# Side steps at every second dense step in three stretches of a four-branch encoder layer

## The chip, the cores and the metric

One core of one Trainium2 chip runs the whole program. The time is in device microseconds (us) of one execution; the number given for a kernel is the median of three runs. PE is TensorE (matmuls, with PEld its weight loads), DVE is VectorE, ACT is ScalarE, POOL is GpSimd, SP is SyncE, which issues the DMAs here.

## The reference

Two groups of 512 tokens (`x_prompt`, `x_sample`) go through the same two layers. In fp32, with D = 1024:

```
h = rms_norm(x, g_mix);  z = h @ w_in          # one projection, split into 15 parts
A = retention(rq, rk, rv) * silu(rg)           # 4 heads, chunks of 128, both directions
B = neighbourhood_attention(nq, nk, nv) * silu(ng)   # 8 heads, 8x16 window, learned bias
C = rg_lru(conv(lx)) * silu(lg)                # both directions
D = hgrn2(hq, hff, hfb, hi) * silu(hg)         # 4 heads, both directions
x = x + (sum over j of sigmoid(h @ w_mg[j]) * (branch_j @ w_br[j])) @ w_o
x = x + sigmoid(rms_norm(x, g_ple) @ w_pg) * (p @ w_pp)
```

After the second layer a last RMSNorm gives the two outputs.

## The kernel before

The kernel makes four passes through `layer`: group 0 and group 1 through layer 0, then both through layer 1. Activations lie with their channels on the partitions, 128 by 512 a tile. Every fp32 operand of a large product is split into a high and a low part (`split`, L246: ACT writes `hi`, DVE writes `lo`), and a product is three matmuls (`mm3`, L275). Weights come as units of 128 by 1024 (512 KB): `weights` (L261) issues the DMA into `wr` (two buffers) and splits it into `wh` by ACT and `wl` by DVE (three buffers each). One unit feeds 24 matmuls of 512 columns; half of it, 12 matmuls, is a dense step.

The order of PE's instructions is the order in which the program issues them (`manual_schedule` for PE, L1239). The order on ACT, DVE, POOL and SP is set when the program is built, by a scheduler with its own estimate of times; each of these engines then works through its list in that order.

Branches are generators that yield after each step. `mix` (L1078) runs a dense generator, and after each of its steps gives every side generator a credit; a whole credit takes one side step. So `mix` writes PE's order. The parts that matter here, in one pass:

- `a_proj` (L611) is dense: `vproj` (eight steps, RV, its units two steps each) and four `ztile` units for q and k, 16 steps in all. Beside it runs `b_core` (L843), the core of branch B, at 1.15 steps to a dense step. One step of it has been taken before: the query tile of the first pair.
- `b_core` takes for each of four head pairs: the query tile and the key tile (`b_qk`, L749, 24 matmuls each, evicted from PSUM by ACT into the high part and by DVE into the low part of `nqk`), then the scores in two steps (`b_scores`, L773, 12 small matmuls each, which read both parts), and behind the second the softmax (`b_soft`, L793, on ACT and DVE). Transposes and value products of a pair (`b_pair`, L826) are taken between the steps of the next pair; for the first pair there is nothing between.
- `vproj` for HI and `c_proj` (L872) are dense, 16 steps; `b_core` goes on at 1.6.
- `merge` for branch B (L948, 24 dense steps) has `a_core` (L653) beside it at 1.0 and the first head of `d_core` (L509) at 0.35.

PSUM has four banks for dense tiles (`mm`) and four for side steps (`co`).

Of the kernel before, what the change touches and what calls it, by code (L numbers as in the profile page):

```python
# [91 lines left out]
class Trunk:  # L92
# [982 lines left out]
                    self.nc.sync.dma_start(out=self.dbg[name][n, i], in_=bo[n][:, i].bitcast(F32))  # L1075

    @staticmethod
    def mix(dense, *sides):  # L1078

        credit = [0.0] * len(sides)  # L1080
        for _ in dense:
            for i, (gen, rate) in enumerate(sides):
                credit[i] += rate
                while credit[i] >= 1.0:
                    credit[i] -= 1.0
                    next(gen, None)
# [7 lines left out]
    def layer(self, g, l, nxt, prev, start=None):  # L1094
        chain = itertools.chain
        sa, sb_, sc, sd = {}, {}, {}, {}
        a, b, c, d, dst = [], [], [], [], []
        self.mg, self.mhl = [None] * 8, [None] * 8

        if start is None:  # L1100
            self.mix(self.b_proj(l, sb_), (prev, 0.3))
        else:
            self.mix(self.b_proj(l, sb_, True), (start, 1.0))
            self.drain(start)
        bcore = self.b_core(l, sb_, b)
        next(bcore)
        self.mix(self.a_proj(l, sa), (bcore, 1.15), (prev, 0.7))
        self.mix(chain(self.vproj(l, C_HI, sd), self.c_proj(l, sc)), (bcore, 1.6), (prev, 0.7))
        self.drain(prev)
        self.drain(bcore)  # L1110
        self.show("B", b)
        acore = self.a_core(l, sa, a)
        self.mix(self.d_proj(l, 0, dst), (acore, 0.9))
        self.cops = {}
        self.c_fetch(l, 0, sc["X"])
        ccore = chain(*[self.c_tile(l, t, sc["X"], c) for t in range(4)])
        dcore = [self.d_core(l, n, dst, sd["V"], d) for n in range(4)]
        self.mix(self.merge(l, 1, b, True, False), (acore, 1.0), (dcore[0], 0.35))
        self.drain(acore)
        self.show("A", a)  # L1120
        self.mix(self.d_proj(l, 1, dst), (dcore[0], 1.0), (ccore, 0.62))
        self.mix(self.merge(l, 0, a, False, False), (chain(dcore[0], dcore[1]), 0.5), (ccore, 0.62))
        self.mix(self.d_proj(l, 2, dst), (chain(dcore[0], dcore[1]), 0.6), (ccore, 0.62))
        self.drain(dcore[0], ccore)
        self.show("C", c)
        self.mix(self.d_proj(l, 3, dst), (dcore[1], 0.6), (dcore[2], 0.4))
        self.mix(self.merge(l, 2, c, False, False), (chain(dcore[1], dcore[2]), 0.5), (dcore[3], 0.4))
        gt = []
        self.mix(self.gates(l, 3, gt), (chain(dcore[1], dcore[2], dcore[3]), 0.6))
        self.drain(*dcore)  # L1130
        self.show("D", d)
        self.mix(self.merge(l, 3, d, False, True, gt), (self.late, 1.0))
        self.drain(self.late)
        st = {}
        self.p_load(g, l, st)
        side = iter(()) if nxt is None else self.make_h(*nxt)
        self.mix(self.w_out(g, l, st), (side, 0.5))
        self.drain(side)
        self.drain(self.ple(g, l, st))
        return self.close(g, l, st)  # L1140
# [110 lines left out]
```

## Time and profile before

| | |
|---|---|
| median of three runs | 3078.2 us (3077.31 to 3078.43) |
| the profiled execution, its own time | 3077.61 us |
| its span, first to last instruction | 3075.8 us |
| mean granted TensorE clock | 0.996 |
| PE busy | 3038.0 us, 17940 matmuls |
| DVE, ACT, POOL busy | 1864.3, 1346.7, 635.5 us |

The profiled execution is one run with the profiler on. Its own time is 1.8 us above its span and 0.6 us under the median. A matmul of 512 columns is shown as 0.39 us long, while the next one starts 0.227 us later: their records overlap, so a busy share near 100% says only that PE is not idle. What a stretch takes is read from the start times. Four stretches of the trace repeat each other, one for each pass; they begin about 757 us apart.

### The profile page before, as it was taken

The page shows a single profiled execution, that of the slowest core. Times are in us where ns is not written, and L with a number is a line of the kernel's source. Part 1 is how long each engine was busy: PE and PEld are TensorE (multiplying, and loading weights), DVE is VectorE, ACT ScalarE, POOL GpSimd, SP SyncE. Part 2 cuts the span into 40 slices and gives each one's busy share as a digit, 9 for nine tenths or more (in the row PEclk, how much of TensorE's full clock was granted, in tenths as well). Part 3 has the DMA queues.
Part 4 walks back from the last instruction along what each step waited for, and adds up shares of the span by engine and source line. Part 5 has one row for each costly group of instructions (what it writes and reads, how often), then busy time and mean ns, then how long its engine had stood idle before and what let it go on. Part 6 is the DMA issues. An engine that isn't in the chain of part 4 may idle for free.

```text
span 3075.8 us, 44900 instructions
## 1 busy us (share of the span) xinstructions
PE 3038.0 (99%) x17940; PEld 2463.9 (80%) x17940; DVE 1864.3 (61%) x2864; ACT 1346.7 (44%) x2173; POOL 635.5 (21%) x486
## 2 busy tenths in 40 slices
PE   8999999999999999999999999999999999999997
PEld 6888877888888887788888887788887888778886
DVE  7556667457455665745646666574665666666446
ACT  4433464344343346433433335643453433564333
POOL 3102043232120113311112112231201211223120
PEclk9999999999999999999999999999999999999998
DMA  5423222244432222223443322222435332222232
GB/s 169 125 92 95 81 93 89 78 145 152 154 116 91 88 93 88 84 85 130 144 147 116 97 83 93 84 87 83 147 106 169 112 96 83 93 81 90 84 131 74
DMA packets 115105, 326.57 MB, mean 106 GB/s; under 512 B 20816, under 2 KB 25680, under 8 KB 114896
## 3 DMA queue, kind: packets, MB, share of 16 engines
q1 hardware_dynamic: 114896, 323.70, 32.4%
q8 instruction: 141, 2.31, 0.3%
q14 instruction: 68, 0.56, 0.1%
HBM read 298.48 MB, written 12.58 MB: 101 GB/s over the span
## 4 chain that ended last, share of the span: by engine, by line
PE 97%; DVE 1%; ACT 1%; DMA 1%; POOL 0%; issue 0%; SPq 0%; DVEq 0%; POOLq 0%; ACTq 0%
PE z L277 22%; PE z L278 22%; PE z L279 21%; PE bp L277 4%; PE bp L279 4%; PE bp L278 4%; PE v L277 3%; PE v L278 3%; PE v L279 3%; PE bo L821 1%; PE cg L912 1%; PE bs L785 1%; PE bt L809 1%; PE by L506 1%; PE ks L587 1%; PE ss L322 1%
## 5 line engine op out<-in xcount | busy, mean ns | idle before, releaser
L250 DVE TENSOR_TENSOR wl<-wr,wh 128x1024 fp32r<-128x1024 f32 x487 | 628.1, 1290 | 679.3 <-ACT wh L248 675.1
L248 ACT ACTIVATE wh<-wr 128x1024 fp32r<-128x1024 f32 x488 | 516.3, 1058 | 1090.2 <-PE z L278 773.1
L277 PE MATMUL z<-hh,wh 128*128 128x512 f32 x2432 | 967.7, 398 | 0.0
L278 PE MATMUL z<-hl,wh 128*128 128x512 f32 x2432 | 948.4, 390 | 2.4 <-DVE hl L250 2.4
L279 PE MATMUL z<-hh,wl 128*128 128x512 f32 x2432 | 948.8, 390 | 0.0
L277 PEld LDWEIGHTS z<-hh,wh 128*128 128x128 f32 x2432 | 457.0, 188 | 117.8 <-issue 22.2
L279 PEld LDWEIGHTS z<-hh,wl 128*128 128x128 f32 x2432 | 456.9, 188 | 96.9
L278 PEld LDWEIGHTS z<-hl,wh 128*128 128x128 f32 x2432 | 457.4, 188 | 92.1 <-DVE hl L250 2.8
L978 POOL TENSOR_TENSOR mg<-mg,mt 128x512 f32<-128x512 f32 x96 | 144.0, 1503 | 448.1 <-DVE mt L976 448.1
L544 POOL TENSOR_TENSOR K<-K,f 128x512 f32<-128x512 f32 x112 | 146.4, 1308 | 434.3 <-DVE f L548 314.6
L277 PE MATMUL v<-wh,hh 128*128 128x512 f32 x384 | 155.5, 405 | 8.2 <-ACT wh L248 8.2
L278 PE MATMUL v<-wl,hh 128*128 128x512 f32 x384 | 152.2, 396 | 0.5 <-DVE wl L250 0.5
L279 PE MATMUL v<-wh,hl 128*128 128x512 f32 x384 | 151.8, 395 | 0.0
L768 POOL TENSOR_TENSOR bm<-run,cmask 128x256 f32<-128x256 f32 x96 | 79.1, 858 | 318.8 <-DMA run<-rpb 203.0
L353 POOL TENSOR_TENSOR acc<-acc,sq 128x512 f32<-128x512 f32 x52 | 80.3, 1544 | 266.3 <-ACT sq L352 262.8
L545 DVE TENSOR_TENSOR Q<-Q,f 128x512 f32<-128x512 f32 x112 | 91.8, 819 | 67.9 <-PE by L506 20.9
L278 PE MATMUL z<-mhl,wh 128*128 128x512 f32 x256 | 100.0, 391 | 0.9 <-DVE mhl L252 0.9
L277 PE MATMUL z<-mhl,wh 128*128 128x512 f32 x256 | 100.0, 391 | 0.4
L277 PE MATMUL z<-h2h,wh 128*128 128x512 f32 x256 | 99.6, 389 | 0.0
L279 PE MATMUL z<-h2h,wl 128*128 128x512 f32 x256 | 99.6, 389 | 0.0
L279 PE MATMUL z<-mhl,wl 128*128 128x512 f32 x256 | 99.6, 389 | 0.0
L278 PE MATMUL z<-h2l,wh 128*128 128x512 f32 x256 | 99.6, 389 | 0.0
(254 smaller groups left out, 4628.5 us busy)
## 6 DMA issues: line engine op xcount, KB each, us to landing
wr<-wu SPq DMA_DIRECT2D x488, 512.0 KB
vb<-vs SPq DMA_DIRECT2D x32, 256.0 KB
run<-rpb SPq DMA_DIRECT2D x32, 244.5 KB
vs<-V SPq DMA_DIRECT2D x4, 1024.0 KB
sw<-raw SPq DMA_DIRECT2D x32, 128.0 KB
qq<-raw SPq DMA_DIRECT2D x32, 128.0 KB
xs<-X SPq DMA_DIRECT2D x32, 128.0 KB
xo<-xT SPq DMA_DIRECT2D x16, 256.0 KB
```

The costliest lines, as they stand in the source:

```text
L248: nc.scalar.activation(hi, src, AF.Copy, scale=scale)
L250: (eng or nc.vector).tensor_sub(lo, src, hi.bitcast(F32))
L277: t.matmul(out, lhsT=wh, rhs=xh, start=start, stop=False)
L278: t.matmul(out, lhsT=wh, rhs=xl, start=False, stop=False)
L279: t.matmul(out, lhsT=wl, rhs=xh, start=False, stop=stop)
L322: nc.tensor.matmul(c, lhsT=self.onesr, rhs=x, start=i == 0, stop=i == 1)
L353: (eng or nc.gpsimd).tensor_tensor(out=acc, in0=acc, in1=s, op=ALU.add)
L506: self.nc.tensor.matmul(bank[r0:r0 + 32, col + 32 * (b // 4):col + 32 * (b // 4) + 32], lhsT=kf(32 * b), rhs=qf(32 * b), start=True, stop= ...
L544: nc.gpsimd.tensor_tensor(out=kv, in0=kv, in1=tk, op=ALU.mult)
L545: nc.vector.tensor_tensor(out=qv, in0=qv, in1=tq, op=ALU.mult)
L768: nc.gpsimd.tensor_tensor(out=bm[:, ty].rearrange("p (r j) -> p r j", j=32), in0=self.view(run, 488 - off, [[-63, 8], [-1, 32]]), in1=self ...
L978: nc.gpsimd.tensor_add(self.mg[m], self.mg[m], dst)
```

## The change

`mix` gets a parameter `every`. With `every=2` the side generators are given twice the credit after the first, third, fifth (and so on) dense step, and nothing after the others. Three calls use it: beside `a_proj`, beside `vproj` and `c_proj`, and beside the merge of branch B. In the last one the rate of `d_core` is 0.4 in place of 0.35.

```diff
     @staticmethod
-    def mix(dense, *sides):
+    def mix(dense, *sides, every=1):
 
         credit = [0.0] * len(sides)
-        for _ in dense:
+        for n, _ in enumerate(dense):
+            if n % every:
+                continue
             for i, (gen, rate) in enumerate(sides):
-                credit[i] += rate
+                credit[i] += rate * every
                 while credit[i] >= 1.0:
                     credit[i] -= 1.0
                     next(gen, None)
...
-        self.mix(self.a_proj(l, sa), (bcore, 1.15), (prev, 0.7))
-        self.mix(chain(self.vproj(l, C_HI, sd), self.c_proj(l, sc)), (bcore, 1.6), (prev, 0.7))
+        self.mix(self.a_proj(l, sa), (bcore, 1.15), (prev, 0.7), every=2)
+        self.mix(chain(self.vproj(l, C_HI, sd), self.c_proj(l, sc)), (bcore, 1.6), (prev, 0.7), every=2)
...
-        self.mix(self.merge(l, 1, b, True, False), (acore, 1.0), (dcore[0], 0.35))
+        self.mix(self.merge(l, 1, b, True, False), (acore, 1.0), (dcore[0], 0.4), every=2)
```

## Rows read from the trace of the kernel before

**Rows 1.** The page, busy us of each engine (share of the span).

```profile
PE 3038.0 (99%) x17940; PEld 2463.9 (80%) x17940; DVE 1864.3 (61%) x2864; ACT 1346.7 (44%) x2173; POOL 635.5 (21%) x486
```

**Rows 2.** The page, chain that ended last, share of the span by engine.

```profile
PE 97%; DVE 1%; ACT 1%; DMA 1%; POOL 0%; issue 0%; SPq 0%; DVEq 0%; POOLq 0%; ACTq 0%
```

**Rows 3.** Waits of PE, whole span: releaser, us in total, times, longest.

```profile
PE v L277 <- ACT wh L248: 8.2, 1, 8.2
PE ss L322 <- ACT sh L248: 7.8, 2, 4.9
PE bs L785 <- ACT nqk L248: 2.5, 1, 2.5
...
```

**Rows 4.** Timeline, second pass, first key tile to scores: start us, us, engine, line.

```profile
814.06 0.39 PE L277 MATMUL z<-hh,wh 128*128 128x512 f32 x1
...
814.52 0.39 PE L279 MATMUL z<-hh,wl 128*128 128x512 f32 x1
814.72 1.06 ACT L248 ACTIVATE wh<-wr 128x1024 fp32r<-128x1024 f32 x1 [6.62 <-PE z L278]
814.74 0.39 PE L277 MATMUL v<-wh,hh 128*128 128x512 f32 x1
...
815.68 0.58 ACT L248 ACTIVATE nqk<-z 128x512 fp32r<-128x512 f32 x1
815.81 1.23 DVE L250 TENSOR_TENSOR wl<-wr,wh 128x1024 fp32r<-128x1024 f32 x1 [6.33 <-ACT wh L248]
...
816.95 0.68 DVE L250 TENSOR_TENSOR nqk<-z,nqk 128x512 fp32r<-128x512 f32 x1
...
817.55 1.01 PE L785 MATMUL bs<-nqk 64*128 64x256 f32 x12
...
818.50 0.50 PE L277 MATMUL v<-wh,hh 128*128 128x512 f32 x1
```

**Rows 5.** Timeline of PE, the same place in the fourth pass.

```profile
2328.84 0.39 PE L277 MATMUL v<-wh,hh 128*128 128x512 f32 x1
...
2334.18 0.39 PE L785 MATMUL bs<-nqk 64*128 64x256 f32 x2 [2.46 <-ACT nqk L248]
2335.55 1.22 PE L785 MATMUL bs<-nqk 64*128 64x256 f32 x10 [0.99 <-DVE nqk L250]
2336.70 0.79 PE L277 MATMUL v<-wh,hh 128*128 128x512 f32 x1
...
2340.84 0.99 PE L785 MATMUL bs<-nqk 64*128 64x256 f32 x12
2341.76 0.50 PE L277 MATMUL v<-wh,hh 128*128 128x512 f32 x1
...
2344.60 0.39 PE L277 MATMUL z<-hh,wh 128*128 128x512 f32 x1
```

**Rows 6.** Timeline of ACT, the same place in the fourth pass.

```profile
2332.59 1.06 ACT L248 ACTIVATE wh<-wr 128x1024 fp32r<-128x1024 f32 x1 [6.95 <-DMA wr<-wu]
2333.55 0.58 ACT L248 ACTIVATE nqk<-z 128x512 fp32r<-128x512 f32 x1
```

**Rows 7.** Stretch behind that wait: PE, PEld, DVE, ACT, POOL busy, PEclk, DMA, GB/s.

```profile
2335.90:2339.20 3.30, 3.30 (x16) 2.59 (x13) 2.02 (x3) 0.00 (x0) 0.00 (x0) 0.50 0.92 239
```

**Rows 8.** Timeline of PE, a wait in the first pass, 23 matmuls between.

```profile
42.19 0.79 PE L278 MATMUL z<-hl,wh 128*128 128x512 f32 x1 [2.40 <-DVE hl L250]
...
49.07 0.39 PE L277 MATMUL v<-wh,hh 128*128 128x512 f32 x1
```

**Rows 9.** Timeline, second pass, end of third softmax and its transposes.

```profile
909.79 1.14 DVE L803 TENSOR_SCALAR S<-S,sm 128x256 f32<-128x256 f32 x4
...
911.57 1.03 PE L809 MATMUL bt<-ident,S 128*128 128x128 f32 x8
```

**Rows 10.** Timeline, first pass, one level of the branch D head.

```profile
393.16 0.46 PE L506 MATMUL by<-Q,kc 128*32 128x32 f32 x32
...
395.92 0.62 ACT L499 ACTIVATE kc<-K 128x512 f32<-128x512 f32 x1
```

## The prediction

> **What bounds the kernel now.** I read the page first: PE is busy 3038.0 of 3075.8 us [rows 1], and the chain that ended last is PE for 97% [rows 2]. Then the list of PE's waits: the reader should see that its two longest rows, 8.2 and 7.8 us, are the first weights and the sums of squares at the two ends of the program, and that the third, 2.5 us ahead of a score step, is one wait inside it [rows 3]. Because matmul records overlap, I then went to the timeline and read start times: dense matmuls start every 0.227 us (0.68 us for three) [rows 4]. In the stretches that the change touches, PE starts one instruction behind the other with no wait, but for that one place in the fourth pass. So moving steps about can win almost nothing; what it can do is put an instruction of PE ahead of the data that it needs. The question for each new neighbourhood is: what does the step wait for, and how much PE work used to lie between.
>
> **What the change moves.** Walking through the generators by hand gives PE's order. In `a_proj` and `vproj`/`c_proj` the credits are the same in sum (8 x 2.3 = 16 x 1.15, 8 x 3.2 = 16 x 1.6). Beside the merge `a_core` takes the same 18 steps, and `d_core` nine in place of eight. Nothing is added or taken out: no matmul, no eviction, no DMA. The order in which weight units are fetched stays the same in all three stretches (only behind them the gate unit of the first D head comes before a unit of `d_proj`), so SP's queue and its transfers are passed by nothing new that I can find.
>
> **The one step that loses its cover.** Now the first pair's key tile is followed by a dense step (RV, second half of unit 0) and then by its first scores. After the change the credit of 2.3 behind dense step 0 takes key tile and scores back to back, and the dense step comes behind both. For later pairs the steps of the pair before lie between key tile and scores, and two dense steps too, so it happens once in each pass. What the scores wait for is in rows 4: key tile's last matmul at 814.52; ACT first splits a weight unit (814.72, 1.06 us; that buffer is freed by the key tile's last but one matmul) and then evicts the key tile (815.68, 0.58); DVE does the same in the same order and has the low part at 816.95 + 0.68 = 817.63. The scores start at 817.55. The dense step between, 12 x 0.227 = 2.7 us, thus covers the eviction to within a tenth of a microsecond. Without it the scores end no earlier than they do now, at 818.50, since ACT and DVE set that end, and the 12 matmuls follow behind it: **+2.7 us a pass**. Queued behind the waiting scores on PE is everything else, all of it in program order, so nothing can fill the hole. In the fourth pass ACT's split waits for a late weight transfer and the eviction stands behind it [rows 6]; PE waits already [rows 5], for a time that PE does not set, so there too the dense step is pushed behind: +2.7. Four passes: **+10.9 us**.
>
> The order on ACT and DVE is not in the diff; the scheduler makes it anew. If the eviction went first, the high part would be there at 814.52 + 0.39 + 0.58 = 815.5 and the low part 0.68 later, at 816.2; the scores, free to start at 814.8, want it from 815.0 on: a wait of 1.2 us in place of 2.7. I take 2.7, because in rows 4 and rows 6 the split goes first, and its buffer will still be freed a matmul before the key tile is complete. The ends are 1.2 and 2.7.
>
> **The clock.** After the wait of 2.46 and 0.99 us in the fourth pass [rows 5] PE ran at a granted clock of 0.50, which is 1.2 GHz [rows 7]: the dense step took 4.14 us (2336.70 to 2340.84) against 2.84 us for the next one (2341.76 to 2344.60), so 1.3 us lost. After 2.40 us of idling in the first pass 23 matmuls took 6.88 us against 5.22, so 1.7 lost [rows 8]. The new wait is 1.5 us for the high part (814.8 to 815.68 + 0.58), two score matmuls, then 1.1 us for the low part (to 817.63), near to these. I take 1.4 us for each of the first three passes, **+4.2 us**, with 0 and 1.7 as ends; the fourth pays its fall already. The Trainium skill (TensorE: Matmul & The Clock Gate, "Why this matters for your kernels") lets the clock fall only after longer gaps between matmuls than this one; by it this term would be nil. The 2.40 us gap above, with the fall behind it, speaks against the rule.
>
> **Fewer switches.** A dense step behind small matmuls takes 2.84 in place of 2.72 us [rows 5]: a switch back costs 0.12 us. I count 70 returns a pass in place of 75, but where two small groups now touch, their own change of tile eats most of it (scores behind value products wait as long as dense steps behind them); I take 0.25 us a pass, **-1.0 us**, with 0 and -2.4 (5 x 0.12 x 4) as ends.
>
> **What keeps its cover.** Softmax to transposes: the last normalising step is done before the transposes start, at the tightest of the sixteen places by 0.64 us (909.79 + 1.14 to 911.57) [rows 9]. The PE work between is the same after the change (a query tile and two dense steps), in another order: the tile comes first, so its eviction (0.58 on ACT, 0.68 on DVE) falls into the softmax, where it fell behind it. 0.68 against 0.64, and the second head's transposes come half a microsecond later still: I take 0. If the unit split (1.23 on DVE) also gets ahead, the wait is 0.68 + 1.23 - 0.64 = 1.3 us, for 12 of the softmaxes. Weights: a unit can be split when the third one back is released; the shortest such cover falls from about 10 us (three dense steps and two score steps of 1 us) to 6.4 us (two dense steps and a step of transposes), against 2.3 us of splitting (814.72 to 815.81 + 1.23) [rows 4]. The D head's levels come every two dense steps (5.4 us) beside the merge; a level needs 395.92 + 0.62 - 393.16 = 3.4 us [rows 10], hidden; bare it would be 3.4 us for each of seven levels. The two score and two local products of branch A now fill all four side banks, and the next level waits for the first to be evicted: 0 to 0.5 us a pass, I take 0.
>
> **Sum.** 10.9 + 4.2 - 1.0 = +14.1 us. On the profiled execution's 3077.6 us that is 3091.7; the median is 0.6 higher, so **3092.3 us**.
>
> **Rivals.**
> Eviction first (not slower): if the scheduler puts the key tile's eviction ahead of the split on ACT and DVE, three passes pay 1.2 us with no fall of the clock, and the fourth gains: its 2.46 + 0.99 + 1.3 = 4.75 us go, for 1.2 at the scores and some 0.8 at the next unit, whose low part still lands at 2332.59 + 1.09 + 1.23 = 2334.9 and is wanted at 2334.1. Sum 3.6 - 2.75 - 1.0, about 0: 3078 us. What decides is the first ACT instruction behind the key tile. For it: the eviction is issued earlier in the program. Against it: all four passes show the split first.
> No fall of the clock: as forecast without the 4.2: 3088.1 us. For it: the new wait is broken by two matmuls; against it: the 2.40 us gap.
> Softmax late: 12 x 1.3 = 15.6 us on top, 3108 us. For it: the slack of 0.64; against it: over the whole stretch ACT and DVE have the same work as now.
> A gain from longer dense runs: the Trainium skill (Perfetto Trace Analysis, "Matmul Optimizations") asks for matmuls back to back in batches. As a mechanism here it is the switches (-2.4 us) and the end of the fourth pass's wait (-4.75): 3071.0 us at the very best, and it needs the scores not to wait at all. Rows 4 speak against that.
>
> **Chances.** Forecast 0.67, no fall 0.07, softmax late 0.06, eviction first 0.15, gain 0.05. A run of this kernel tells about 0.2% from no change, 6.2 us here: the first three are slower (0.80), eviction first is the same, and of the gain I give 0.04 to faster and 0.01 to same. The forecast's own range is 3086 (no fall in some passes, 2.4 from switches) to 3099 (1.7 a fall, half a microsecond a pass at the banks, some late transposes). Alone it holds too little, so the range goes down to eviction first: 3078 to 3101.
>
> **What would show it.** In the list of waits: score matmuls (bs) waiting for nqk four times from ACT, about 1.5 us each in three passes, and four times from DVE, about 1.1; granted clock 0.50 behind each; the first scores ending where they end now (818.50 in the second pass, plus what the first has lost), with a dense step behind them. ACT's timeline behind the key tile: split, then eviction. Waits of the transposes (bt) on DVE would show the softmax rival; new waits beside the merge would show a cover that I missed. I am wrong if the eviction goes first, if PE waits for weights, or if the stretch beside the merge changes by more than 1 us.

## The result and the profile after

The changed kernel takes 3096.6 us (median of four runs, 3093.3 to 3099.8) where the kernel before took 3078.0 beside it (3077.3 to 3078.4): 1.0060 times the time, with a 95% interval of 1.0048 to 1.0073. It is slower by 18.6 us; 14.1 were predicted. The profiled execution is one of the two long ones (3099.6 us, span 3097.8, mean granted clock 0.994), so its own account has to give 22.0 us.

The page after, busy us of each engine and the chain that ended last:

```profile
PE 3043.7 (98%) x17940; PEld 2469.1 (80%) x17940; DVE 1847.9 (60%) x2864; ACT 1347.4 (43%) x2173; POOL 627.5 (20%) x486
...
PE 96%; DVE 2%; ACT 1%; DMA 1%; issue 0%; POOL 0%; SPq 0%; DVEq 0%; POOLq 0%; ACTq 0%
```

The counts of instructions are those of [rows 1] to the last one: nothing was added. PE is busy 5.7 us longer with the same matmuls, and the chain [rows 2] has lost a point of PE to DVE. So the 22 us are PE standing still, and PE running slower behind it. The list of PE's waits in the changed kernel says where (engine, line, releaser; us in total, times, longest):

```profile
PE bs L785 <- ACT nqk L248: 9.1, 4, 4.8
...
PE al L702 <- ACT kk L674: 5.1, 4, 1.3
PE bs L785 <- DVE nqk L250: 3.8, 4, 1.0
...
```

Against [rows 3] two things are new. The scores (`bs`) wait for the key tile's high part four times in place of once, and for its low part as often. And `al`, a product of branch A beside the merge, waits 1.3 us for `kk` in each pass. No row of the list is a transpose (`bt`), and the rows left out are of the kinds that the kernel before has too.

**At the scores, second pass.** The timeline of the changed kernel, all engines (start us, length us, engine, line; in brackets the idle time before and its releaser), is to be laid beside [rows 4]:

```profile
820.80 0.39 PE L279 MATMUL z<-hh,wl 128*128 128x512 f32 x1
821.00 1.06 ACT L248 ACTIVATE wh<-wr 128x1024 fp32r<-128x1024 f32 x1 [6.62 <-PE z L278]
...
821.96 0.58 ACT L248 ACTIVATE nqk<-z 128x512 fp32r<-128x512 f32 x1
822.09 1.23 DVE L250 TENSOR_TENSOR wl<-wr,wh 128x1024 fp32r<-128x1024 f32 x1 [6.33 <-ACT wh L248]
822.59 0.39 PE L785 MATMUL bs<-nqk 64*128 64x256 f32 x2 [1.41 <-ACT nqk L248]
823.23 0.68 DVE L250 TENSOR_TENSOR nqk<-z,nqk 128x512 fp32r<-128x512 f32 x1
823.97 0.87 PE L785 MATMUL bs<-nqk 64*128 64x256 f32 x10 [0.99 <-DVE nqk L250]
824.77 0.50 PE L277 MATMUL v<-wh,hh 128*128 128x512 f32 x1
825.70 0.63 PE L277 MATMUL v<-wh,hh 128*128 128x512 f32 x1
826.13 0.63 PE L278 MATMUL v<-wl,hh 128*128 128x512 f32 x1
```

ACT and DVE do what they did before, in the same order and at the same distances: split, then eviction. From the key tile's last matmul to the dense matmul behind the scores it is 3.97 us (820.80 to 824.77), and it was 3.98 (814.52 to 818.50). Only the dense step that lay inside it is now behind it. (In the first and third passes the distance is 4.58 and 4.54 us: there the clock fell while the scores were still running, and their last ten matmuls took 1.44 us in place of 0.87.) The last two rows show the second loss: dense matmuls start 0.43 us apart where 0.227 is usual. The windows behind three of the four waits, those of the first, second and fourth pass (us; then PE, PEld, DVE, ACT, POOL busy; granted clock, DMA share, GB/s):

```profile
60.79:64.20 3.41, 3.17 (x14) 2.63 (x15) 1.47 (x3) 0.00 (x0) 0.00 (x0) 0.50 0.73 192
825.40:828.80 3.40, 3.40 (x10) 2.64 (x9) 0.83 (x2) 0.00 (x0) 0.00 (x0) 0.50 0.54 167
...
2351.20:2357.90 6.70, 5.91 (x22) 4.52 (x23) 2.54 (x4) 0.00 (x0) 0.00 (x0) 0.50 0.50 147
```

The clock is 0.50, the 1.2 GHz level, behind each (in the third pass too, for 3.4 us), where before it was so behind the fourth alone [rows 7], and there for 3.3 us in place of 6.7.

**The fourth pass**, ACT and PE of the changed kernel, to be laid beside [rows 5, 6]:

```profile
2349.53 1.06 ACT L248 ACTIVATE wh<-wr 128x1024 fp32r<-128x1024 f32 x1 [6.75 <-DMA wr<-wu]
2350.49 0.58 ACT L248 ACTIVATE nqk<-z 128x512 fp32r<-128x512 f32 x1
...
2351.13 0.58 PE L785 MATMUL bs<-nqk 64*128 64x256 f32 x2 [4.84 <-ACT nqk L248]
2352.50 1.43 PE L785 MATMUL bs<-nqk 64*128 64x256 f32 x10 [0.80 <-DVE nqk L250]
```

The late weight transfer holds the split, the split holds the eviction, and the wait of 2.46 us has grown to 4.84 because the dense step that lay in front of it is now behind.

**Beside the merge, first pass**, all engines of the changed kernel:

```profile
282.37 0.39 PE L322 MATMUL ss<-sh,onesr 128*128 128x512 f32 x1
282.83 0.60 PE L669 MATMUL at<-ident,raw 128*128 128x128 f32 x4
...
290.44 0.63 ACT L248 ACTIVATE boa<-ot 128x512 fp32r<-128x512 f32 x1 [2.28 <-DVE ot L388]
290.98 1.55 ACT L674 ACTIVATE kk<-at,kdec 128x256 f32<-128x256 f32 x4
291.85 2.05 PE L702 MATMUL al<-V,kk 128*128 128x128 f32 x16 [1.27 <-ACT kk L674]
```

And the same place of the kernel before, ACT and PE:

```profile
277.60 0.39 PE L322 MATMUL ss<-sh,onesr 128*128 128x512 f32 x1
...
280.81 0.60 PE L669 MATMUL at<-ident,raw 128*128 128x128 f32 x4
...
284.48 0.63 ACT L248 ACTIVATE boa<-ot 128x512 fp32r<-128x512 f32 x1 [2.64 <-DVE ot L388]
285.01 1.55 ACT L674 ACTIVATE kk<-at,kdec 128x256 f32<-128x256 f32 x4
...
288.46 1.95 PE L702 MATMUL al<-V,kk 128*128 128x128 f32 x16
```

`kk` was complete at 286.56, 1.9 us ahead of `al`; now `al` starts while `kk` is being written and waits. In both kernels `kk` runs directly behind `boa`, the split of the output of the head before. What has moved is that head's norm (`ss`): it used to be one dense step ahead of the transposes (`at`), and now stands directly in front of them. The way from that norm to `boa` has become longer too, 8.07 us (282.37 to 290.44) in place of 6.88 (277.60 to 284.48): on DVE, steps of the branch D head now run between the norm's own.

Laying the start times of the two traces beside each other gives the account of the 22.0 us: 4.2, 4.3, 4.2 and 3.4 from key tile to scores and just behind (16.1); -0.28 a pass over the rest of branch B's core (-1.1); +1.5 a pass from the merge to the end of the pass (+6.1); and some 0.9 at the start of the program, ahead of anything that the change touches.

### The profile page after: what moved, and what is told of

Read it like the earlier page. It is cut to its first block, busy times and chain, and to the rows that moved or that the text cites. A ratio compares the mean times of both kernels' runs of the same rounds, so it can differ in the third digit from the quotient of the medians.

```text
span 3097.8 us, 44893 instructions
## 1 busy us (share of the span) xinstructions
PE 3043.7 (98%) x17940; PEld 2469.1 (80%) x17940; DVE 1847.9 (60%) x2864; ACT 1347.4 (43%) x2173; POOL 627.5 (20%) x486
## 4 chain that ended last, share of the span: by engine, by line
PE 96%; DVE 2%; ACT 1%; DMA 1%; issue 0%; POOL 0%; SPq 0%; DVEq 0%; POOLq 0%; ACTq 0%
PE z L277 22%; PE z L278 21%; PE z L279 21%; PE bp L277 4%; PE bp L278 4%; PE bp L279 4%; PE v L277 3%; PE v L279 3%; PE v L278 3%; PE bo L821 1%; PE cg L912 1%; PE bs L785 1%; PE bt L809 1%; PE by L506 1%; PE ss L322 1%; PE ks L587 1%
## 5 line engine op out<-in xcount | busy, mean ns | idle before, releaser
L250 DVE TENSOR_TENSOR wl<-wr,wh 128x1024 fp32r<-128x1024 f32 x487 | 616.5, 1266 | 706.4 <-ACT wh L248 705.4
L768 POOL TENSOR_TENSOR bm<-run,cmask 128x256 f32<-128x256 f32 x96 | 68.5, 750 | 285.0 <-DMA run<-rpb 263.7
L489 POOL TENSOR_TENSOR ks<-K 128x512 f32<-128x512 f32 x16 | 41.6, 2602 | 287.4 <-ACT cu L920 218.6
```

The costliest lines, as they stand in the source:

```text
L250: (eng or nc.vector).tensor_sub(lo, src, hi.bitcast(F32))
L489: nc.gpsimd.tensor_add(ks, K[:, 0], K[:, 1])
L768: nc.gpsimd.tensor_tensor(out=bm[:, ty].rearrange("p (r j) -> p r j", j=32), in0=self.view(run, 488 - off, [[-63, 8], [-1, 32]]), in1=self ...
```

## The experiments

Three theories had to be told apart. The forecast's: all the loss is the lost cover at the first pair's scores, with the clock falling behind it. Its extension, from the list of waits: the merge costs a part of its own, through `kk`. And that the clock is no part of it.

**Each call alone.** `e1_proj_a` keeps `every=2` in the call beside `a_proj`, `e2_proj_c` in the one beside `vproj` and `c_proj`, `e3_merge` (with the rate 0.4) in the one beside the merge; the other two calls are as before. For `e1_proj_a`, against the changed kernel:

```diff
-        self.mix(chain(self.vproj(l, C_HI, sd), self.c_proj(l, sc)), (bcore, 1.6), (prev, 0.7), every=2)
+        self.mix(chain(self.vproj(l, C_HI, sd), self.c_proj(l, sc)), (bcore, 1.6), (prev, 0.7))
...
-        self.mix(self.merge(l, 1, b, True, False), (acore, 1.0), (dcore[0], 0.4), every=2)
+        self.mix(self.merge(l, 1, b, True, False), (acore, 1.0), (dcore[0], 0.35))
```

> Every second dense step beside a_proj alone; the other two calls as before. Theory (the first pair's scores lose the dense step that covered the key tile's eviction: 2.65 us of waiting and a fall of the clock of some 1.5 us in each pass, as the changed kernel's trace has it, 4.2 us a pass and 3.4 in the fourth): 3078 + 16 = 3094 us, 3090 to 3096 with fewer falls, four waits of bs for nqk. Rival (the loss is spread over all bursts of side steps): a third of the whole, about 3084 us.

> Every second dense step beside vproj and c_proj alone. Theory (no step there loses its cover, and one switch fewer between small and large matmuls): 3077 to 3078 us, no new wait of PE. Rival (bursts of three side steps wait for evictions, banks or weights by themselves): 3082 to 3084 us with new waits of bs, bt or z.

> Every second dense step beside the merge of branch B alone, with the rate of 0.4. Theory (the local products of branch A's second head pair wait 1.3 us for kk, which ACT evicts behind the split of the head before): 3078 + 6 = 3084 us, al waiting for kk four times, no wait of bs but the one of before. Rival (that wait comes only behind the delays ahead of it in the pass): 3078 us and no wait of al.

Measured beside a kernel before at 3078.5 us: 3092.9 (ratio 1.0046, 1.0031 to 1.0061), 3078.3 (0.9999, 0.9990 to 1.0009) and 3084.4 (1.0018, 1.0009 to 1.0027). That is +14.4, -0.2 and +5.9 us, 20.1 together against 18.6 for the whole change, which is within the intervals. The waits divide in the same way. `e1_proj_a` has the four waits of the scores and none of `al`; `e3_merge` the reverse, with one wait of the scores, the old one of the fourth pass:

```profile
PE al L702 <- ACT kk L674: 5.1, 4, 1.3
...
PE bs L785 <- ACT nqk L248: 2.0, 1, 2.0
...
```

So the extension holds: two separate losses, 14 us in the projections of branch A and 6 beside the merge, and a middle call that costs nothing.

**The cover given back.** `e4_eased` is the changed kernel, but in `a_proj` only the key tile is taken behind the first dense step, and its scores behind the second:

```diff
-    def mix(dense, *sides, every=1):
+    def mix(dense, *sides, every=1, ease=False):
...
-            if n % every:
+            if n % every and not (ease and n == 1):
                 continue
             for i, (gen, rate) in enumerate(sides):
-                credit[i] += rate * every
+                credit[i] += 0.0 if n % every else rate * every
                 while credit[i] >= 1.0:
                     credit[i] -= 1.0
                     next(gen, None)
+                    if ease and n == 0:
+                        break
```

> The changed kernel, but behind the first dense step of a_proj only the key tile is taken and its scores behind the second; all else at every second step. Theory (this one neighbourhood is the loss of the first stretch): waits of bs as before (the fourth pass alone), 3096.6 - 16 + the 4.75 of the fourth pass that before has too; all in all 3078 + 6 - 1 = 3083 us, the rest being kk. Rival (other neighbours of the bursts cost too): over 3088 us.

Measured: 3083.1 us (1.0015, 1.0005 to 1.0024). The scores wait only where they did before (2.1 and 1.0 us, fourth pass); `al` still waits 5.1. One dense step, put back between two side steps, is worth some 14 us (18.6 less 4.6).

**The eviction made shorter.** `e5_evict` is the changed kernel with the first pair's key tile evicted by DVE alone, so that it stands behind neither of ACT's two jobs; `e10_evict_before` is the same edit in the kernel before:

```diff
-        self.split(z, hi, lo)
+        if pair == 0 and base == C_NK:
+            self.nc.vector.tensor_copy(hi, z)
+            self.nc.vector.tensor_sub(lo, z, hi.bitcast(F32))
+        else:
+            self.split(z, hi, lo)
```

> The changed kernel, with the first pair's key tile evicted by DVE alone (high part by a copy, low part behind it), so that no weight split of ACT stands ahead of it. Theory (the scores wait for the eviction behind the split): about 1.3 us of waiting in each pass in place of 2.4, seldom a fall of the clock, and in the fourth pass no wait for the late weight transfer: 3 x 1.3 - 2.6 - 1.1 + 6 over before, 3084.5 us, up to 3088 if the clock still falls. Rival (the scores wait for something else, banks or the query tile): 3096 us as the changed kernel.

> The kernel before, with the first pair's key tile evicted by DVE alone. Theory (in the fourth pass the eviction waits on ACT behind a split whose weights come late): the waits of bs there go, 2.0 to 2.5 and 1.0 us with the fall of the clock, some 0.8 us come back at the next unit: 3078.3 - 3.5 = 3075 us. Rival (the late transfer itself holds PE a moment later): within 1 us of before.

Measured for `e5_evict`: 3086.8 us (1.0028, 1.0017 to 1.0038). Its timeline in the second pass:

```profile
818.56 1.06 ACT L248 ACTIVATE wh<-wr 128x1024 fp32r<-128x1024 f32 x1 [6.62 <-PE z L278]
818.78 0.69 DVE L758 CAST nqk<-z 128x512 fp32r<-128x512 f32 x1 [5.47 <-PE z L279]
...
819.51 0.69 DVE L759 TENSOR_TENSOR nqk<-z,nqk 128x512 fp32r<-128x512 f32 x1
819.62 0.39 PE L789 MATMUL bs<-nqk 64*128 64x256 f32 x2 [0.88 <-ACT wh L248]
820.26 0.87 PE L789 MATMUL bs<-nqk 64*128 64x256 f32 x10 [0.25 <-DVE nqk L759]
```

The wait is 0.88 + 0.25 = 1.1 us in place of 2.4 (the releaser named in the first bracket is ACT's split, but what the two matmuls read is DVE's copy), and the clock falls behind none of the four. This is close to what the rival "eviction first" would have been, though that rival left the high part to ACT. With the 5.9 us of `e3_merge` taken off the 8.5 measured, 2.6 us are left for the four passes, where the rival had about 0; the intervals are too wide to tell these apart. In the fourth pass a new wait came up, 1.2 us of the second pair's scores. The built program did not choose this order.

`e10_evict_before` came out at 3078.0 (1.0000, 0.9991 to 1.0009) where a gain of 3.5 us was expected for the fourth pass. The first pair's scores wait there no longer (from the key tile's last matmul to the second scores it is 6.95 us in place of 12.23), and PE, now earlier, meets the next things that are late. A line from the waits of `e10_evict_before`, two places in its timeline, of ACT and of PE, and the window behind the second:

```profile
PE bs L789 <- DVE nqk L250: 1.6, 1, 1.6
...
2348.58 1.06 ACT L248 ACTIVATE wh<-wr 128x1024 fp32r<-128x1024 f32 x1 [5.85 <-DMA wr<-wu]
...
2352.35 0.63 PE L813 MATMUL bt<-ident,S 128*128 128x128 f32 x4 [3.24 <-DVE S L807]
...
2352.30:2355.70 3.40, 3.35 (x17) 2.86 (x18) 2.43 (x5) 1.70 (x4) 0.00 (x0) 1.00 0.80 209
```

The transposes of the first softmax wait 3.24 us, since the next late weights hold ACT's list, and the second head's softmax behind them, all the same; the second pair's scores then wait 1.6 us for their low part. A wait that a late transfer causes moved here when one of its victims was helped. The granted clock stayed at 1.00 behind the 3.24 us.

**Idling filled with work.** `e6_fill` is the changed kernel with eleven 512-column matmuls, into a side bank that nothing reads, between the first pair's key tile and its scores. If only the lost cover mattered it would change nothing; if the clock falls because PE idles, the time must come down though work is added.

```diff
+                if pair == 0 and base == C_NK:
+                    w = self.co("fill")
+                    for i in range(11):
+                        self.nc.tensor.matmul(w, lhsT=self.hh[:, 0, 0:128], rhs=self.hl[:, 0], start=i == 0, stop=i == 10)
```

> The changed kernel, with eleven matmuls more behind the first pair's key tile, into a side bank that nothing reads (added work, 2.5 us of PE a pass). Theory (part of the loss is the clock that falls behind the wait, 1.5 us): PE is busy while the eviction runs, in three passes the scores wait little and the granted clock stays at 1.00 behind them; 3096.6 - 3 x 1.5 = 3092 us although work is added, and less scatter. Rival (the clock has no part, or the wait is not for the eviction): the 2.5 us come on top or the time stays: 3096 to 3106 us.

Measured: 3094.8 us (1.0055, 1.0041 to 1.0068). By the medians that is 1.8 us under the changed kernel, less than the two intervals can separate, so the time alone proves nothing. The rows say more: PE in the second pass, and the window behind the scores.

```profile
819.82 2.65 PE L855 MATMUL fill<-hl,hh 128*128 128x512 f32 x11
822.40 1.23 PE L785 MATMUL bs<-nqk 64*128 64x256 f32 x12
...
825.00:829.00 4.00, 4.00 (x19) 3.21 (x18) 1.25 (x2) 1.06 (x1) 0.00 (x0) 1.00 0.36 110
```

In the first three passes the scores no longer wait and the clock is 1.00 where it was 0.50. In the fourth a wait of 2.7 + 1.0 us and a fall stay, as the kernel before has them, since the late transfer outlasts the filling. From the key tile's last matmul to the second scores the four places take 2.72, 2.67, 2.67 and 2.64 us more than before: the lost cover as forecast, with no fall added.

**Why `kk` is late.** The first theory was that `kk` stands behind `boa` in ACT's list. `e7_kk` is the changed kernel with the second head pair's `kk` written by DVE:

```diff
+                if pair == 1:
+                    nc.vector.tensor_scalar(out=self.view(kk, T * e + 64 * d, [[128, 4], [1, 64]]),
+                                            in0=self.view(pt, 64 * e, [[128, 4], [1, 64]]),
+                                            scalar1=self.kdec[:, col:col + 1], scalar2=None, op0=ALU.mult)
+                    continue
```

> The changed kernel, with the scaled key copies kk of branch A's second head pair made by DVE in place of ACT. Theory (kk stands in ACT's list behind the split of the head before, whose norm is not done): no wait of al, 3096.6 - 6 = 3091 us. Rival (kk waits for a free buffer, whatever engine writes it): al waits 1.3 us as before and the time stays at 3096 us.

Measured: 3096.3 us (1.0062, 1.0047 to 1.0078), nothing gained. The wait has changed its releaser and is still there, 0.8 us in each pass in place of 1.3; the list of waits, and DVE and ACT in the first pass:

```profile
PE al L707 <- DVE kk L675: 3.0, 4, 0.8
...
289.40 0.85 DVE L388 TENSOR_TENSOR ot<-ot,rf 128x512 f32<-128x512 f32 x1
290.18 1.64 DVE L675 TENSOR_SCALAR kk<-at,kdec 128x256 f32<-128x256 f32 x4
290.29 0.63 ACT L248 ACTIVATE boa<-ot 128x512 fp32r<-128x512 f32 x1 [2.28 <-DVE ot L388]
```

The transposes that `kk` reads were done by about 283.4, and yet DVE begins it only when `boa` can begin too. So it isn't ACT's list; that theory fell. (In DVE's list it stands behind the same norm.) What `kk` and `boa` share is the set of fourteen equal buffers from which `boa`, `qq` and `kk` are taken. `f2_owntag` is the changed kernel with a buffer for `kk` alone, and one less in the set:

```diff
-        return self.sb.tile([P, 2, T], dt, tag="k4", name=name, bufs=14)
+        return self.sb.tile([P, 2, T], dt, tag="k4", name=name, bufs=13)
...
-        qq, kk = self.k4("qq"), self.k4("kk")
+        qq = self.k4("qq")
+        kk = self.sb.tile([P, 2, T], F32, tag="kk", name="kk", bufs=1)
```

> The changed kernel, with a buffer of its own for the scaled key copies kk (and thirteen in place of fourteen shared ones). Theory, in place of the one that fell with the copies on DVE (the shared buffers are handed out in the program's order, so kk gets its buffer when the split of the head before gets its own, though others are free): ACT writes kk right behind the transposes, no wait of al, 3096.6 - 5.5 = 3091 us. Rival (kk is late for another reason): al waits 1.3 us as before, 3096 us; or thirteen shared buffers are too few and new waits come up elsewhere.

Measured: 3092.5 us (1.0044, 1.0030 to 1.0057), and no wait of `al` is left. Its timeline, first pass:

```profile
281.67 1.57 ACT L675 ACTIVATE kk<-at,kdec 128x256 f32<-128x256 f32 x4 [2.31 <-PE at L670]
288.64 0.63 ACT L248 ACTIVATE boa<-ot 128x512 fp32r<-128x512 f32 x1 [2.28 <-DVE ot L388]
288.71 2.05 PE L703 MATMUL al<-V,kk 128*128 128x128 f32 x16
```

`kk` now runs seven microseconds ahead of `boa`, right behind the transposes. That sharing the set is the cause is shown. Why sharing it delays `kk` is not: it may be the order of handing out (program order, `boa` first), as the expectation has it, or a lack of free buffers at that moment. `f2_owntag` made the set smaller by one but took `kk` out of it as well, so it does not tell the two apart, and no run gave the set more buffers.

**The clock, seen in runs made for something else.** `e7_kk` and `f2_owntag` leave the scores as the changed kernel has them, and their waits are the same, 1.41 to 1.46 and 0.99 us in the first three passes. In the second pass of `e7_kk` the clock did not fall, as this window behind the scores shows:

```profile
824.60:828.00 3.40, 3.40 (x16) 2.82 (x15) 0.91 (x2) 0.90 (x1) 0.00 (x0) 1.00 0.56 160
```

Measured as for `e6_fill`, that pass costs 2.67 us over the kernel before, the lost cover alone. The first and third passes of `e7_kk`, with a fall of 3.4 and one of 6.8 us, cost 4.17 and 5.54. In the first pass of `f2_owntag` the clock did not fall either, and the cost is 2.72. So the clock's part is real, and whether it is charged differs between executions of the same wait: ten of the twelve such waits in `after`, `e1_proj_a`, `e7_kk` and `f2_owntag` had a fall behind them.

**Does the account close?** `g2_eased_own` is the changed kernel with both cures, those of `e4_eased` and `f2_owntag`.

> The changed kernel with both losses mended: the first scores behind the second dense step, and kk with a buffer of its own. Theory (these two are the whole loss): 3083.1 - 6 = 3077 us, within 1.5 us of the kernel before. Rival (something else is left): over 3080 us.

Measured: 3077.6 us beside 3078.5 (0.9997, 0.9988 to 1.0006). The waits in the stretches of the change are those of the kernel before and no others. The 18.6 us are these two places; what the fewer switches bring, 0.9 us by the medians, is too little to be told from nothing.

**A faster kernel?** The last wait left in these stretches is the fourth pass's late weights. `g3_late_y` is the kernel before with the last norm and the eight output transfers of group 0, which run beside the projections of the fourth pass, put behind them; `g1_best` has `every=2` in the first two calls too, the first eased.

```diff
...
-        self.mix(self.a_proj(l, sa), (bcore, 1.15), (prev, 0.7))
...
+        self.mix(self.a_proj(l, sa), (bcore, 1.15), *[(prev, 0.7)] * (nxt is not None))
...
```

> The kernel before, with the last norm and the eight output transfers of group 0 issued behind the projections of the fourth pass, in place of beside the projection of branch B. Theory (these transfers and their waits on SP make the weights late that the fourth pass's scores wait for): the waits of bs go, 2.5 + 1.0 + 1.3 us, 3078.3 - 4.7 = 3073.5 us. Rival (the weights are late for another reason, or the outputs hold something up where they now go): 3078 us or more.

> As the run with late outputs, and every second dense step beside a_proj (its first scores eased) and beside vproj and c_proj; the merge as before. Theory (fewer switches between large and small matmuls, 0.25 us a pass): 1 us less than with late outputs alone, 3072.5 us. Rival: the bursts cost something that the trace did not show: 3074 us or more.

Measured: 3081.1 us (1.0008, 0.9999 to 1.0017) and 3080.8 (1.0007, 0.9999 to 1.0016), where 3073.5 and 3072.5 were expected. The scores' waits do go in the fourth pass, and that place is 5.3 us shorter (12.23 to 6.97). But the outputs now stand on SP's queue ahead of the table of distances for the next stretch. The waits of `g3_late_y`, then SP's queue, DVE, and a window of that place:

```profile
PE z L277 <- DVE S L691: 6.9, 1, 6.9
...
2504.64 3.98 SPq L1068 DMA_DIRECT2D yT<-y  x6
2508.71 0.59 SPq L637 DMA_DIRECT2D dist<-dist  x1
2512.10 1.89 DVE L642 TENSOR_SCALAR band<-dist,lgam 128x128 f32<-128x128 f32 x4 [2.69 <-DMA dist<-dist]
...
...
2512.00:2525.70 13.70, 6.83 (x19) 5.11 (x18) 11.79 (x24) 5.44 (x13) 8.21 (x9) 0.63 0.31 93
```

PE is busy for 6.83 of 13.70 us there, at a mean granted clock of 0.63: the 5.3 us won at the scores are spent, and more. No version measured beats the kernel before by more than its interval.

## Why the prediction was right, and where it was short

**The lost cover, +10.9 us: right.** The step was "the scores end no earlier than they do now ... and the 12 matmuls follow behind it". In the second pass the distance from key tile to next dense matmul stayed at 3.97 us, and where no fall was added the place costs 2.64 to 2.72 us (the four passes of `e6_fill`, 10.7 together; one pass each of `e7_kk` and `f2_owntag`).

**Order on ACT and DVE: right.** Split, then eviction, in all four passes, as [rows 4, 6] had it. `e5_evict` shows what hung on it.

**The clock, +4.2 us: right in place, its size in part luck.** In the profiled execution the fall came behind each of the three new waits and cost 1.4, 1.6 and 1.5 us where 1.4 was taken. In the fourth pass, where nothing more was charged, it cost another 0.7. That is 5.2 us, but the same waits cost 6.4 in `e1_proj_a`, 4.4 in `e7_kk` and 2.7 in `f2_owntag`, since falls were missing or twice as long: 4.2 was a fair middle, not a property of the wait. The changed kernel's four runs lie 6.5 us apart where the one before lies within 1.1, and the two long ones have the lowest mean clock (0.994); that the number of falls makes this difference is likely, but only the profiled run shows its falls one by one. The rule of the Trainium skill by which this term would be nil (TensorE: Matmul & The Clock Gate, "Why this matters for your kernels") is not borne out: 1.41 and 0.99 us of idling, with two matmuls between, had a fall behind them in ten of twelve places.

**Fewer switches, -1.0 us: right in size.** In the changed kernel's trace the rest of branch B's core is 0.28 us shorter a pass; no run shows this gain by itself (`e2_proj_c` and `g2_eased_own` are within their intervals of no change). That is also the most that the batches asked for by the Trainium skill (Perfetto Trace Analysis, "Matmul Optimizations") were worth here.

**What keeps its cover: right for softmax, weights and the D head.** No transpose waits, in any pass, and no new row of PE waiting for weights.

These terms together were +14.1 us; the changed kernel with only the wait of `kk` taken away (`f2_owntag`) is 14.0 above the kernel before, and the first call alone (`e1_proj_a`) 14.4. That they agree to a few tenths is closer than the falls of the clock allow one to count on.

**The merge, 0 us: wrong.** The step that failed is the last of "what keeps its cover": "the two score and two local products of branch A now fill all four side banks ... 0 to 0.5 us a pass, I take 0". Only the banks were weighed there. For the local product itself the question put at the head of the prediction, what does it wait for and what lay between, wasn't asked: it waits for `kk`, and `kk` for `boa`, and the dense step between the head's norm and the transposes was that chain's cover. Asked of the trace of before, it has an answer: `kk` was done 1.9 us ahead of `al`, and a dense step of 2.7 us was taken out of the way to it. 2.7 - 1.9 = 0.8 would have been nearer to the 1.3 measured than 0; the 1.2 us by which the way from the norm to `boa` grew are not in that sum. With what the waits upset behind them the merge cost 1.5 us a pass, 5.9 in all (`e3_merge`), over the bound of 1 us that the prediction itself had set for being wrong there.

The forecast fell 4.3 us short of the median, near enough all of it in that one term; its range and its sign held.

## What to carry to other kernels

When side steps are bunched, look at each pair that becomes adjacent: read from the trace when the later one's operand is complete, including what stands ahead of its producer in an engine's list and in the set of buffers it is taken from, and compare the margin with the work taken out of between. Each of these two places needed only one dense step or one buffer to be healed (`g2_eased_own`), and where a wait comes from a late transfer, helping one of its victims moves it to the next. On PE, reckon with slower matmuls behind a wait as well: here ten of twelve like waits had them, at 1.4 to 2.9 us each.

## What the runs showed of the hardware

The granted clock fell to 0.50, for 3.4 or 6.8 us, behind waits of 1.41 to 1.46 and 0.99 us with two small matmuls between them in ten of the twelve places where the traces have them. It stayed at 1.00 in the other two (the second pass of `e7_kk`, the first of `f2_owntag`), behind 0.88 and 0.25 us in all four passes of `e5_evict`, behind each wait of 1.27 us at `al`, and also behind 2.10 and 0.99 us (`e4_eased`) and a single wait of 3.24 (`e10_evict_before`). So the length of a wait alone does not tell here whether a fall follows.

With eleven matmuls that nothing reads in the gap, the window behind the scores had 1.00 in place of 0.50 (`e6_fill`), in three passes of three, for 2.65 us of matmuls that would otherwise have been mostly waiting. With falls in ten of twelve places without the filling, three without a fall are likely its doing, though chance is not quite excluded.
